# First query groups beside the even layer's last unit, a new order for the first unit, and later weight loads behind the y pieces

## The chip, the cores and the metric

One core of a Trainium2 chip runs the whole program in one launch. The metric is device time in microseconds. Engines are called as the profile calls them: PE (TensorE, matmuls), PEld (its weight loads), DVE (VectorE), ACT (ScalarE), POOL (GpSimd) and SP (SyncE, which issues nearly all DMAs). Every engine works through its own instructions in the order in which they were put, so an instruction that waits holds all that stand behind it.

## The reference

One inference step of two layers over a prompt of 2048 rows and 32 sample rows (8 sequences of 4 tokens), model width 1024, float32. Layer 0 runs HGRN2 heads and forgetting-attention heads in parallel from one input projection; layer 1 is gated linear attention.

```python
h = rmsnorm(x, norm_even)                   # layer 0
qa, fa, ia, ga, qb, kb, vb, gb, fb = split(h @ w_in_even)      # eight blocks of 512 columns, fb has 4
f = lb + (1 - lb) * sigmoid(fa)
o_a = gated_linear_chunked(qa, 1 - f, ia, log(f))              # 4 heads of 128, state in and out
o_b = forgetting attention (qb, kb, vb, log_sigmoid(fb + b_fox)):
    c = cumsum(log_f)
    prompt: softmax(q k^T * 128**-0.5 + c_t - c_s, s <= t) @ v          # 2048 queries, 4 heads
    sample: the same over 2048 paged past rows per sequence (128 pages of k, 128 of v) and 4 new ones
x = x + concat(head_rmsnorm(o_a) * silu(ga), o_b * silu(gb)) @ w_out_even
h = rmsnorm(x, norm_odd)                    # layer 1: GLA, 4 heads, key 128, value 256
x = x + (head_rmsnorm(gla(h @ w_in_odd)) * silu(g)) @ w_out_odd
y = rmsnorm(x, final_norm)
```

Outputs are y, the new keys, values and log forgets, and the states.

## The kernel before, in words

**Float32 from half-precision matmuls.** Every float32 operand is scaled by a power of two and split into a high and a low half in 16 bits; a product takes three matmuls (`mm3`, L476: hi·hi, hi·lo, lo·hi, lines 478 to 480). A weight unit is 256 columns: `half_unit` (L315) loads the raw block (`wr_…`), *measures* its largest value (four reduces `rm_…` on DVE, one small matmul `spr_…` that spreads it over the partitions, four tiny DVE steps), and *splits* it into `w_…` on ACT, DVE and POOL.

**Even layer** (`phase_even`, L958). The prompt is taken in two halves of 1024 rows; the sample's 32 rows go with the first. `norm_groups` (L408) loads row tiles (`nx_…`), squares them on ACT (`nsq`), scales them on DVE, transposes them on PE (`nt_…`) and splits the result into `act`. Then 16 units of projection per half run in a fixed order: v0, g0, qf0, qf1, …, Bk0, Bv0, Bk1, Bv1 (in the trace `pt_Av`, `pf_Ag`, `pf_A…`, …, `pt_Bk`, `pt_Bv`). `staged` (L1070) hands one unit's pieces to PE and between them fetches, measures and splits the units to come, by a list `todo`: for unit 0 of the first half it names unit 1's steps and, after the last piece, unit 2's measure, scale and split. `handover` (L452) mixes the norm of the row tiles with unit 0's pieces. `few_rows` (L510) does the sample's rows (`pS_…`) from a copy of their columns (`sam_…`, DVE). `more_consts` (L159) prepares constants (`lb`, `wgr`, `scT`, `mlev`) after unit 0. The linear attention of each head is mixed between pieces by `mux`, by costs that the code gives.

**Forgetting attention** (`phase_fox`, L1148). `bias_rows` writes the cumulated log forgets to `cbd`. `fox_prompt` (L1183) goes through 16 groups of 512 queries (4 heads × 4): per block of 128 queries scores `s` (PE), bias and running maximum (DVE, L1233), exponentials (ACT, L1241), normalising (POOL, L1249), transposes `pt` (PE, L1269), halves `th`/`tl` (ACT L1276, DVE L1277) and values `fo` (PE). The decode stream `fox_sample` (L1336) goes through the 256 pages (256 KB each): transposes `pkt`, copies `kts`, scores `sc`, softmax, values `pv`; its setup splits queries into `qz` on DVE. `until` (L92) alternates the two by the ratio of two numbers, `FOX_P` = 270000 for the prompt's cost and `FOX_S` = 411000 for the sample's, until the sample is through. What is left of the prompt is mixed with `prepare`, the odd layer's first loads.

**Odd layer** (`phase_odd`). `y_pieces` (L1608) load the attention output `yr` and split it into `act`; `row_tiles` load the rows `row_…` to which the output projection adds; `out_units` (units 0 to 3, `pt_o`) multiply by `w_out_even`, whose blocks are `wr_o`. Then norm and the units of layer 1.

**What sets the order.** The kernel records its operations in the order in which the generators yield, and a scheduling layer then places them per engine; inside `tc.issue_after(x)` an operation gets a place behind x. Tile pools give buffers by tag; a pool opened in the place of a closed one waits for its tiles.

## Time and profile before

| | us |
|---|---|
| median of 3 runs | 2395.92 (2392.24 to 2399.04) |
| the profiled execution, its own time | 2394.72 |
| its span, first to last instruction | 2392.4 |
| mean granted TensorE clock in it | 0.986 |

In the profile the even layer lies at 0 to 883 us, the forgetting attention at 883 to 1310, the rest to the end is the odd layer. A row of the timeline gives the start, the duration, engine, line, operation, output and inputs, their shapes, how many were merged, and in brackets how long the engine sat idle before it and what ended that. [...] A row of the busy time by stretch gives for each engine the us of work in the stretch and the instructions, then the granted clock as a share of full speed, the DMA engines' mean busy share and their GB/s.

### The profile page before, as it was taken

The numbers are of one execution on the slowest core, as the hardware profiler recorded it, in microseconds if no ns is written. First come the engines' busy times: TensorE is split into PE (matmuls) and PEld (weight loads), VectorE is DVE, ScalarE is ACT, GpSimd is POOL, SyncE is SP. The second block draws the span as 40 slices with busy tenths as digits, with TensorE's granted clock in tenths as the row PEclk, the third lists the DMA queues.
The fourth block names the chain that finished last, engine by engine and source line by source line (L and its number), as shares of the span: only waits on it lengthen the run. The fifth ranks groups of instructions, "written<-read, shape, count | busy, mean of one in ns | idle before, by whom it ended". The sixth has DMA issues, their size and how long they took to land. (4 is left out here: it accounts for less than half of the span.)

```text
span 2392.4 us, 58667 instructions
## 1 busy us (share of the span) xinstructions
PE 2294.1 (96%) x23324; PEld 1633.7 (68%) x23324; DVE 1417.9 (59%) x3347; ACT 1107.5 (46%) x2458; POOL 753.7 (32%) x843
## 2 busy tenths in 40 slices
PE   6999999999999999999999999999999999999998
PEld 5677677864655875655446876777778766666887
DVE  7566556446655548666767463665675645557554
ACT  5334343342333226556667454535543635545333
POOL 2233222112212225234556211432452222322322
PEclk9999999999999999999999999999999999999999
DMA  6231234535541267676874632122156312114453
GB/s 198 63 88 58 81 113 142 175 92 143 149 136 43 85 192 258 223 251 203 270 241 134 213 109 58 46 81 86 50 151 196 111 41 70 43 59 159 154 192 147
DMA packets 297013, 317.24 MB, mean 133 GB/s; under 512 B 39730, under 2 KB 241011, under 8 KB 296739
## 3 DMA queue, kind: packets, MB, share of 16 engines
q1 hardware_dynamic: 295234, 308.98, 41.1%
q8 instruction: 183, 3.00, 0.5%
q0 software_dynamic: 1504, 4.52, 0.5%
q14 instruction: 92, 0.75, 0.1%
HBM read 242.31 MB, written 71.11 MB: 131 GB/s over the span
## 5 line engine op out<-in xcount | busy, mean ns | idle before, releaser
L480 PE MATMUL pt_o<-w_o,act 128*128 128x256 f16 x1024 | 280.5, 274 | 3.1 <-DVE act L1633 2.9
L478 PE MATMUL pt_o<-w_o,act 128*128 128x256 f16 x1024 | 280.7, 274 | 1.3 <-ACT sg1C L534 1.1
L479 PE MATMUL pt_o<-w_o,act 128*128 128x256 f16 x1024 | 280.5, 274 | 1.0 <-POOL w_o L353 1.0
L480 PEld LDWEIGHTS <-act 128*128 128x128 f16 x2304 | 226.6, 98 | 36.1 <-issue 4.6
L478 PEld LDWEIGHTS <-act 128*128 128x128 f16 x2304 | 226.6, 98 | 36.0 <-ACT act L473 4.0
L479 PEld LDWEIGHTS <-act 128*128 128x128 f16 x2304 | 226.7, 98 | 32.4 <-issue 2.9
L478 PE MATMUL pt_Cv<-w_Cv,act 128*128 128x256 f16 (+1 forms) x512 | 140.3, 275 | 1.7 <-ACT act L473 0.9
L644 POOL TENSOR_TENSOR kA<-kA,fA 128x512 f32<-128x512 f32 (+1 forms) x56 | 79.8, 1425 | 192.6 <-PE gl_A L610 143.0
L479 PE MATMUL pt_Cv<-w_Cv,act 128*128 128x256 f16 (+1 forms) x512 | 140.0, 274 | 0.0
L480 PE MATMUL pt_Cv<-w_Cv,act 128*128 128x256 f16 (+1 forms) x512 | 139.7, 274 | 0.0
L1241 ACT ACTIVATE L<-L,nm,kc 128x512 f32<-128x512 f32 (+3 forms) x160 | 118.2, 741 | 36.9 <-DVE nm L1239 27.2
L644 POOL TENSOR_TENSOR kC<-kC,fC 128x512 f32<-128x512 f32 (+1 forms) x56 | 81.8, 1461 | 148.2 <-PE gl_C L610 101.3
L1249 POOL TENSOR_SCALAR L<-L,nm 128x512 f32<-128x512 f32 (+3 forms) x160 | 98.8, 631 | 70.8 <-DVE nm L1245 28.6
L1276 ACT ACTIVATE th<-pt 128x512 f16<-128x512 f32 (+3 forms) x159 | 80.7, 527 | 59.8 <-PE pt L1269 58.9
L1277 DVE TENSOR_TENSOR tl<-pt,th 128x512 f16<-128x512 f32 (+3 forms) x159 | 94.4, 609 | 20.3 <-ACT th L1276 19.0
L1269 PE MATMUL pt<-ident,L 128*128 128x128 f32 x544 | 91.3, 280 | 4.9 <-DVE tl L1277 2.4
L1269 PEld LDWEIGHTS pt<-ident,L 128*128 128x128 f32 x544 | 66.7, 143 | 32.4 <-DVE tl L1277 9.1
L1393 PEld LDWEIGHTS pkt<-ident,pgcache_fox_k 128*128 128x128 f32 x512 | 58.1, 141 | 44.4 <-issue 25.6
L1393 PE MATMUL pkt<-ident,pgcache_fox_k 128*128 128x128 f32 x512 | 76.1, 279 | 4.7 <-DVE kts L1397 2.0
L478 PE MATMUL pt_Av<-w_Ai,act 128*128 128x256 f16 x256 | 70.9, 277 | 1.9 <-ACT act L473 1.9
L479 PE MATMUL pt_Av<-w_Ai,act 128*128 128x256 f16 x256 | 70.7, 276 | 0.4 <-DVE w_Ai L346 0.4
L478 PE MATMUL pt_Bk<-w_Bk,act 128*128 128x256 f16 x256 | 71.0, 277 | 0.0
(952 smaller groups left out, 6738.3 us busy)
## 6 DMA issues: line engine op xcount, KB each, us to landing
pgcache_fox_k<-in_cache_fox_k SPq DMA_DIRECT2D x128, 256.0 KB, 4.2
pgcache_fox_v<-in_cache_fox_v SPq DMA_DIRECT2D x128, 256.0 KB, 4.2
yr<-yT SPq DMA_DIRECT2D x16, 1024.0 KB, 7.4
nx<-in_x_prompt SPq DMA_DIRECT2D x16, 512.0 KB, 5.4
wr_Aqf<-in_w_in_even SPq DMA_DIRECT2D x64, 128.0 KB, 3.2
wr_o<-in_w_out_even SPq DMA_DIRECT2D x32, 256.0 KB, 4.5
wr_Cv<-in_w_in_odd SPq DMA_DIRECT2D x32, 256.0 KB, 3.8
wr_Cqk<-in_w_in_odd SPq DMA_DIRECT2D x64, 128.0 KB, 2.8
```

Source lines behind the costliest of these rows:

```text
L478: nc.tensor.matmul(ps, lh[0], rh[0], start=first, stop=False)
L479: nc.tensor.matmul(ps, lh[0], rh[1], start=False, stop=False)
L480: return nc.tensor.matmul(ps, lh[1], rh[0], start=False, stop=last)
L644: nc.gpsimd.tensor_tensor(kv[:, :, 0], kv[:, :, 0], t1.to_broadcast([P, nb, w]), ALU.mult)
L1241: self.last_exp = nc.scalar.activation(lt[:, :w], lt[:, :w], AF.Exp, bias=nm[:, 0:1], scale=ib, accum_out=nm[:, 2 + j : 3 + j])
L1249: nc.gpsimd.tensor_scalar(lt[:, :w], lt[:, :w], nm[:, 1:2], 2.0**14, ALU.mult, ALU.mult)
L1269: nc.tensor.transpose(pt[:, w : w + P], rows[b][s // 4][0][:, (s % 4) * P : (s % 4 + 1) * P], self.ident)
L1276: nc.scalar.activation(th[:, a:w], pt[:, a:w], AF.Copy),
L1277: nc.vector.tensor_tensor(tl[:, a:w], pt[:, a:w], th[:, a:w], ALU.subtract)))
L1393: nc.tensor.transpose(pk[:, j * P : (j + 1) * P], pgs[j][:, h * P : (h + 1) * P], self.ident)
```

## The change

Four parts, in the diff's order of lines:

1. **Start.** `warm_up` puts matmuls of the identity with itself, into a PSUM tile that nobody reads, on PE: 9 behind `spr_e`, 4 behind the first transpose, one behind each second transpose of the first group of row tiles. The squares of every second row tile after the first group go to DVE. The row tile `nx_768` is loaded behind the first block `wr_Ag`. Unit 0 gives its first four pieces inside `handover`; then unit 1's first piece is taken (`next(gates)`), then the rest of unit 0. Unit 2's measure, scale and split, and steps of units 3 and 4, stand in unit 1's list; a scale step stands behind the last matmul recorded.
2. **Even layer's end.** `bias_rows` stands behind the second piece of unit Bk1 instead of behind the unit. The pools are split so that those on the left close early; `open_fox` opens the prompt's pools before the last unit Bv1, and `until` mixes prompt work of cost `PRE_P` = 16000 into Bv1's pieces. Two PSUM tags (`kt`, `sc`) are opened later, with the decode stream.
3. **`FOX_P`** is 245000 instead of 270000, so less prompt is handed out per decode step.
4. **Odd layer's start.** The weight loads of `dense(0, 3)` and the row tiles from the third on get a place behind the last load `yr`.

```diff
-FOX_P = 270000.0
+FOX_P = 245000.0
+PRE_P = 16000.0
...
-                    nc.scalar.activation(sq[:n], xt[:n], AF.Square, accum_out=ss[:n])
+                    if share and j and c0 > P:
+                        nc.vector.tensor_tensor_reduce(sq[:n], xt[:n], xt[:n], 1.0, 0.0, ALU.mult, ALU.add, ss[:n])
+                    else:
+                        nc.scalar.activation(sq[:n], xt[:n], AF.Square, accum_out=ss[:n])
...
+            def warm_up(n, after):
+                with tc.issue_after(after.ins):
+                    for _ in range(n):
+                        nc.tensor.matmul(warm[:, :P], self.ident, self.ident, start=True, stop=True)
+
+            warm_up(9, self.last_spread)
...
+                    def each0(st, k, j):
+                        if j or k == 0:
+                            warm_up(1 if j else 4, self.last_t)
+                        if (k, j) == (2, 0):
+                            st.enter_context(tc.issue_after(self.last_scale.ins))
...
-                    first = self.handover(list(zip(steps, turns)), dense(0, 1), last)
+                    first = dense(0, 1)
+                    drain(self.handover(list(zip(steps, turns)), islice(first, 4), last))
+                    gates = dense(1, 3)
+                    next(gates)
                     drain(first)
...
-                drain(dense(1, 3))
+                drain(dense(1, 3) if hf else gates)
...
-                drain(dense(14, 15))
+                keys = dense(14, 15)
                 if hf == 1:
+                    next(keys)
+                    next(keys)
                     self.bias_rows(pps, *masks)
+                drain(keys)
                 last = dense(15, 16)
-            drain(last)
+            left.close()
+            fx = self.open_fox()
+            drain(until(self.prompt, PRE_P, last, cost))
+        self.phase_fox(*fx)
...
+                    if n == 2:
+                        st.enter_context(self.tc.issue_after(self.last_mm.ins))
                     self.ready[u] = us[u][0][n]()
...
-            if j:
+            if j == 1 and beside:
+                todo = [[], [(2, 1), (4, 0)], [(2, 2)], [(2, 3), (3, 1)], [(3, 2)], [(3, 3)]]
+            elif j:
                 todo = [[(j + 3, 0), (j + 2, 1)], [(j + 2, 2)], [(j + 2, 3)]]
...
-                todo = [[(1, 0)], [(1, 1)], [(2, 0), (1, 2), (1, 3)], [(3, 0)], [(2, 1), (2, 2), (2, 3)]]
+                todo = [[(1, 0)], [(1, 1)], [(2, 0), (1, 2), (1, 3)], [(3, 0)]]
...
+                        if first and j > 1:
+                            st.enter_context(tc.issue_after(self.last_yr.ins))
+                        nc.sync.dma_start(t[:m], self.rows(hf, c0, m, first))
...
-            with tc.issue_after(self.last_y.ins):
+            with tc.issue_after(self.last_y.ins), tc.issue_after(self.last_yr.ins):
                 drain(dense(0, 3))
```

**PE, end of unit 0.** Before, the spread of unit 2's measure (`spr_Aqf`) stands between the sample's matmuls of unit 0 (`pS_Av`) and unit 1's first piece (`pf_Ag`):

```order
L522 MATMUL pS_Av_683<-w_Ai_153,sam_Av_680 32x256
L279 MATMUL spr_Aqf_721<-ident,rm_Aqf_715 128x128
L478 LDWEIGHTS w_Ag_577
L478 MATMUL pf_Ag_847<-act,w_Ag_577 128x352
L479 LDWEIGHTS w_Ag_577
```

Now unit 1's first piece begins among the last row tiles of unit 0, before the transposes of the sample's rows are through:

```order
L484 MATMUL pt_Av_648<-w_Ai_169,act 128x256
L483 LDWEIGHTS w_Ag_605
L483 MATMUL pf_Ag_709<-act,w_Ag_605 128x352
L484 LDWEIGHTS w_Ag_605
L484 MATMUL pf_Ag_709<-act,w_Ag_605 128x352
L445 MATMUL nt_2_624<-ident,nx_1024_509 128x32
```

The other 22 matmuls of that piece, the 24 of `pS_Av` and two more pieces (48 matmuls) then stand ahead of `spr_Aqf`.

**DVE, the same place.** Before:

```order
L517 COPY sam_Av_680<-act 128x8x32 x2
L292 TENSOR_REDUCE rm_Aqf_715<-wr_Aqf_560 128x1 x4
L165 TENSOR_SCALAR g_hgrn<-g_hgrn 128x4
L165 TENSOR_SCALAR g_gla<-g_gla 128x8
L172 TENSOR_TENSOR lb<-lb 128x4
L191 MEMSET wgr 80x512
L213 CAST mdiag<-ident 128x128
L232 MEMSET scT_833 128x1024
L232 MEMSET scT_834 128x1024
L292 TENSOR_REDUCE rm_Aqf_881<-wr_Aqf_671 128x1 x4
```

Now:

```order
L522 COPY sam_Av_738<-act 128x8x32 x2
L167 TENSOR_SCALAR g_hgrn<-g_hgrn 128x4
L167 TENSOR_SCALAR g_gla<-g_gla 128x8
L174 TENSOR_TENSOR lb<-lb 128x4
L193 MEMSET wgr 80x512
L215 CAST mdiag<-ident 128x128
L234 MEMSET scT_866 128x1024
L234 MEMSET scT_867 128x1024
L175 TENSOR_TENSOR lb<-lb 128x4
L176 TENSOR_TENSOR lb<-lb 128x4
L294 TENSOR_REDUCE rm_Aqf_908<-wr_Aqf_588 128x1 x4
L294 TENSOR_REDUCE rm_Aqf_997<-wr_Aqf_699 128x1 x4
```

Unit 2's reduces have moved behind the constants; seven more rows stand between them and the last small reduce that `spr_Aqf` takes.

**PE, the even layer's last unit.** Before, the first scores stand behind all of Bv1's matmuls:

```order
L480 MATMUL pt_Bv_10895<-w_Bv_10244,act 128x256
L478 LDWEIGHTS h_q_10986
L478 MATMUL s_11002<-h_k_10990,h_q_10986 128x128
L479 LDWEIGHTS h_q_10986
L479 MATMUL s_11002<-l_k_10991,h_q_10986 128x128
```

Now they stand inside, from behind its 54th matmul on:

```order
L485 MATMUL pt_Bv_11007<-w_Bv_10272,act 128x256
L483 LDWEIGHTS h_q_10790
L483 MATMUL s_10806<-h_k_10794,h_q_10790 128x128
L484 LDWEIGHTS h_q_10790
L484 MATMUL s_10806<-l_k_10795,h_q_10790 128x128
```

Counted over the whole order, the prompt's 1546 PE instructions (`s`, `pt`, `fo`) lie so, before and now: ahead of Bv1's last matmul 0 and 62; from there to the first `pkt` 62 and 85; from the first `pkt` to the last `pv` 1260 and 1161; behind it 224 and 238.

**SP, the odd layer's start.** Before (`yr` of 256 columns are 1 MB, `wr_o` and the rows 256 KB and 512 KB each):

```order
L1619 DMA yr_19220<-yT_76 128x8x256
L327 DMA wr_o_19432<-in_w_out_even 128x2x256 x4
L327 DMA wr_o_19542<-in_w_out_even 128x2x256
L1619 DMA yr_19437<-yT_76 128x8x256
L327 DMA wr_o_19542<-in_w_out_even 128x2x256 x3
L327 DMA wr_o_19611<-in_w_out_even 128x2x256 x4
L1619 DMA yr_19449<-yT_76 128x8x256
L1619 DMA yr_19461<-yT_76 128x8x32
```

Now:

```order
L1666 DMA yr_19183<-yT_76 128x8x256
L329 DMA wr_o_19462<-in_w_out_even 128x2x256 x4
L1666 DMA yr_19467<-yT_76 128x8x256
L1666 DMA yr_19479<-yT_76 128x8x256
L1666 DMA yr_19491<-yT_76 128x8x32
L329 DMA wr_o_19572<-in_w_out_even 128x2x256 x2
```

Seven loads `wr_o` stood ahead of the last `yr`; now only unit 1's four do, and the rows come ahead of the last six.

## Rows read from the trace of the kernel before

**Rows 1.** page, part 1: engine, busy us, share of the span, instructions

```profile
span 2392.4 us, 58667 instructions
PE 2294.1 (96%) x23324; PEld 1633.7 (68%) x23324; DVE 1417.9 (59%) x3347; ACT 1107.5 (46%) x2458; POOL 753.7 (32%) x843
```

**Rows 2.** timeline of PE, start: start, us, line, op, [idle before <-releaser]

```profile
8.12 1.11 PE L440 MATMUL nt<-ident,nx 128*128 128x128 f32 x4 [3.82 <-DVE nx L428]
15.85 0.42 PE L480 MATMUL pt_Av<-w_Ai,act 128*128 128x256 f16 x1
19.69 0.29 PE L480 MATMUL pt_Av<-w_Ai,act 128*128 128x256 f16 x1
21.34 0.27 PE L480 MATMUL pt_Av<-w_Ai,act 128*128 128x256 f16 x1
```

**Rows 3.** timeline of PE, end of unit 0 and start of unit 1

```profile
50.67 1.66 PE L522 MATMUL pS_Av<-w_Ai,sam_Av 128*32 128x256 f16 x24 [1.47 <-DVE sam_Av L517]
59.14 0.79 PE L279 MATMUL spr_Aqf<-ident,rm_Aqf 128*128 128x128 f32 x2 [6.82 <-DVE kc L261]
59.73 0.50 PE L478 MATMUL pf_Ag<-act,w_Ag 128*128 128x352 f16 x1
64.11 0.31 PE L478 MATMUL pf_Ag<-act,w_Ag 128*128 128x352 f16 x1
65.90 0.31 PE L478 MATMUL pf_Ag<-act,w_Ag 128*128 128x352 f16 x1
```

**Rows 4.** timeline of DVE beside it

```profile
50.39 0.83 DVE L517 COPY sam_Av<-act 128x256 f16<-128x256 f16 x2
50.73 2.45 DVE L292 TENSOR_REDUCE rm_Aqf<-wr_Aqf 128x1 f32<-128x512 f32 x4
56.08 2.39 DVE L292 TENSOR_REDUCE rm_Aqf<-wr_Aqf 128x1 f32<-128x512 f32 x4
58.95 0.14 DVE L294 TENSOR_REDUCE rm_Aqf<-rm_Aqf 128x1 f32<-128x4 f32 x1
```

**Rows 5.** timelines of DVE and ACT, norm of a row tile

```profile
19.95 0.75 DVE L428 TENSOR_SCALAR nx<-nx,rsr_n 128x1024 f32<-128x1024 f32 x1 [0.66 <-POOL rsr_n L405]
16.16 1.04 ACT L426 ACTIVATE nsq<-nx 128x1024 bf16<-128x1024 f32 x1
```

**Rows 6.** busy by stretch: us, PE PEld DVE ACT POOL, PEclk, DMA share, GB/s

```profile
883.20:901.30 18.10, 14.59 (x65) 7.26 (x63) 12.45 (x55) 10.07 (x26) 11.73 (x19) 0.72 0.95 311
901.30:914.30 13.00, 8.90 (x48) 4.55 (x47) 10.28 (x28) 8.46 (x21) 8.63 (x11) 0.87 0.97 335
914.30:1272.70 358.40, 343.15 (x2441) 196.76 (x2442) 248.64 (x769) 229.09 (x517) 161.94 (x258) 0.99 0.71 231
1272.70:1310.30 37.60, 33.13 (x239) 24.39 (x239) 30.55 (x85) 27.49 (x60) 30.41 (x35) 0.95 0.30 98
```

**Rows 7.** timeline of PE, from the even layer into the forgetting attention

```profile
883.18 0.27 PE L480 MATMUL pt_Bv<-w_Bv,act 128*128 128x256 f16 x1
900.13 0.39 PE L1269 MATMUL pt<-ident,L 128*128 128x128 f32 x2
900.35 0.22 PE L479 MATMUL fo<-tl,h_v 128*128 128x128 f16 x1
901.33 1.04 PE L1393 MATMUL pkt<-ident,pgcache_fox_k 128*128 128x128 f32 x8
909.04 0.22 PE L478 MATMUL s<-h_k,h_q 128*128 128x128 f16 x1 [2.41 <-DVE mx L1233]
```

**Rows 8.** timeline of DVE beside it

```profile
905.74 2.64 DVE L1385 TENSOR_TENSOR qz<-qs,bmask 128x256 f32<-128x256 f32 x4
```

**Rows 9.** timeline of SP's queue, start of the odd layer

```profile
1304.89 7.28 SPq L327 DMA_DIRECT2D wr_o<-in_w_out_even  x7
1313.39 5.76 SPq L1619 DMA_DIRECT2D yr<-yT  x2
```

**Rows 10.** busy by stretch, start of the output projection's second unit

```profile
1330.00:1340.00 10.00, 8.96 (x97) 7.42 (x96) 8.21 (x15) 7.19 (x15) 7.53 (x6) 1.00 1.07 349
```

More of the change, by code (lines that the diff above doesn't have):

```diff
@@ L1 @@
 from contextlib import ExitStack
+from itertools import islice
 import concourse.bass as bass
@@ L262, in spread @@
         ps = pps.tile([P, 512], F32, tag=tag, name=f"spr_{nm}")
-        nc.tensor.matmul(ps[:, :P], m.to_broadcast([P, P]), self.ident, start=True, stop=True)
+        self.last_spread = nc.tensor.matmul(ps[:, :P], m.to_broadcast([P, P]), self.ident, start=True, stop=True)
         nc.vector.reduce_max(t, ps[:, :P], axis=mybir.AxisListType.X)
@@ L429, in prep, with turn @@
                     xs.append(xt)
-            def turn(at=None, then=None):
+            def turn(each=None):
                 c0 = grp[0][0]
@@ L438, in turn @@
                         w = 0
-                        for (_, n), xn in zip(grp, xs):
-                            nc.tensor.transpose(ps[:, w : w + n], xn[:n, k * P : (k + 1) * P], self.ident[:n, :n])
+                        for j, ((_, n), xn) in enumerate(zip(grp, xs)):
+                            self.last_t = nc.tensor.transpose(ps[:, w : w + n], xn[:n, k * P : (k + 1) * P], self.ident[:n, :n])
                             w += n
+                            if each:
+                                each(st, k, j)
                         self.split_evac(ps[:, :w], act[0][:, k, c0 : c0 + w], act[1][:, k, c0 : c0 + w],
                                         gain[:, k : k + 1])
-                        if k == at:
-                            then(st)
             return prep, turn, load
@@ L485, in proj_fm @@
             for k in range(KT):
-                self.mm3(ps[:M, :n], [x[:, k, off : off + M] for x in W],
-                         [x[:, k, c0 : c0 + n] for x in act], k == 0, k == KT - 1)
+                self.last_mm = self.mm3(ps[:M, :n], [x[:, k, off : off + M] for x in W],
+                                        [x[:, k, c0 : c0 + n] for x in act], k == 0, k == KT - 1)
             evac(ps[:M, :n], c0, n)
@@ L971, in phase_even @@
             self.sx_even = self.gain_scale(self.g_even, pps, "pj", "e")
+            warm = pps.tile([P, 512], F32, tag="st", name="warm")
+            def warm_up(n, after):
[3 more added lines that the diff above has]
+            warm_up(9, self.last_spread)
             S1 = sp.tile([P, P], F32, name="Sx")
@@ L1018, in behind, with turn @@
                             groups[g][0]()
[L1020 to L1029 removed]
+                    def each0(st, k, j):
[3 more added lines that the diff above has]
+                            st.enter_context(tc.issue_after(self.last_scale.ins))
+                    def turn0():
+                        groups[0][1](each0)
+                    def turn(t):
+                        groups[t][1](lambda st, k, j: behind(self.last_a, t + 1) if (k, j) == (KT // 2, 0) else None)
+                    steps = [lambda: None, lambda: behind(self.last_split, 1), lambda: None, lambda: None, lambda: None]
+                    turns = [turn0] + [lambda t=t: turn(t) for t in (1, 2, 3)] + [groups[4][1]]
+                    first = dense(0, 1)
+                    drain(self.handover(list(zip(steps, turns)), islice(first, 4), last))
+                    gates = dense(1, 3)
+                    next(gates)
                     drain(first)
+                    first = iter(())
                     with tc.issue_after(self.last_x.ins), tc.issue_after(self.last_a.ins), \
@@ L1146, in log_sigmoid, with open_fox @@
         nc.vector.scalar_tensor_tensor(zz, q, -2.0, zz, ALU.mult, ALU.add)
[L1148 removed]
+    def open_fox(self):
         tc, nc = self.tc, self.nc
         self.fox = ExitStack()
[L1151 to L1164 removed]
@@ new lines, in pool @@
+        def pool(name, **kw):
+            return self.fox.enter_context(tc.tile_pool(name=name, bufs=2, reuse_waits="tile", **kw))
+        f1, f0, pp = pool("fe"), pool("fx"), pool("fpa", space=PSUM)
+        fx = Pool(f0, {"vh": 5, "vl": 5, "P": 17, "th": 4, "tl": 4, "sg": 3, "y": 1},
+                  Pool(f1, {"raw": 6, "caus": 1, "qh": 2, "ql": 2, "kh": 5, "kl": 5, "cb": 2, "st1": 12, "cm": 2}))
+        more = Pool(None, {"kt": 2, "sc": 1})
+        pps = Pool(pp, {"t": 2, "o": 1, "s": 2}, more)
@@ new lines, in open_fox, with phase_fox @@
+        caus = fx.tile([P, P], F32, tag="caus", name="caus")
+        nc.gpsimd.memset(caus, 0.0)
+        nc.gpsimd.affine_select(caus, caus, [[-1, P]], ALU.is_ge, FAR, base=0, channel_multiplier=1)
+        self.prompt = self.fox_prompt(fx, pps, caus)
+        return pps, more
+    def phase_fox(self, pps, more):
+        tc = self.tc
+        more.pool = self.fox.enter_context(tc.tile_pool(name="fpb", bufs=2, space=PSUM, reuse_waits="tile"))
+        with tc.tile_pool(name="fs", bufs=1, side="right", reuse_waits="tile") as s0:
+            fs = Pool(s0, {"pg": PG, "kt": 8})
+            drain(until(self.prompt, FOX_P, self.fox_sample(fs, pps), FOX_S))
@@ L1862, in row_tiles @@
                     t = wp.tile([P, HALF + TS], F32, tag="c4" if j < OC4 else "sg", name=f"row{hf}_{j}")[:, :D]
-                    nc.sync.dma_start(t[:m], self.rows(hf, c0, m, first))
+                    with ExitStack() as st:
+                        if first and j > 1:
+                            st.enter_context(tc.issue_after(self.last_yr.ins))
+                        nc.sync.dma_start(t[:m], self.rows(hf, c0, m, first))
                     r.append(t)
```

48 lines of the change are left out of this document (15 added, 33 removed).

## The prediction

> **What bounds the kernel now.** [...] A matmul of 256 columns costs 0.213 us at the lower level (18 steps from 15.85 to 19.69) and 0.110 at the upper one (15 steps to 21.34) [rows 2]. Three places stand out. At the start PE waits 3.82 us for the first row tile and begins unit 0 at the lower level [rows 2]. At the end of unit 0 it waits 1.47 us for `sam_Av`, then 6.82 us at `spr_Aqf`, and unit 1 begins at the lower level: 0.292 us a matmul of 352 columns for 15 steps, then 0.149 for 12 [rows 3]. Between the even layer and the decode stream the granted clock is 0.72 for 18 us and 0.87 for 13 more [rows 6], with a wait of 2.41 us in them [rows 7]. Beside the decode stream PE is busy 343.15 of 358.4 us, DVE 248.64, ACT 229.09, the DMA engines 0.71 [rows 6]: PE is the limit there, nothing else is near.
>
> **Part 1, the start.** *The stall.* `spr_Aqf` needs the last reduce of unit 2's measure, which DVE ends at 59.09 after working since 50.39 on the sample's copies, eight big reduces and the constants between them [rows 4]. The change does not shorten that work; it puts it behind other PE work. DVE's 8.7 us from the copies to that reduce become about 10 (the order shows `wg`, a sum and unit 1's first product ahead of it now; I put 1.3 on them, about two steps of a 128x512 reduce at 0.6 [rows 4]). PE has in that time `pS_Av` (1.66) and 48 matmuls of 0.149, so 1.66 + 7.15 = 8.8 us, beginning 0.3 us behind the copies. So PE arrives some 0.9 us early: of 1.47 + 6.82 = 8.29 us I take 1 as coming back, 7.3 are won (5.8 to 8.3). The 22 matmuls of unit 1's first piece ahead of `pS_Av` (3.3 us) cover the 1.47.
> *The clock behind it.* Without the stall the 15 slow steps cost 15 x (0.292 − 0.149) = 2.1 us less (0 to 2.1): the clock fell in that stall and in nothing else near it.
> *The warm-up.* Nine identity products are two passes each of 0.213 us at the lower level, 3.8 us in all, beside a wait of 3.82 [rows 2]: they delay nothing. In the two places where a lower clock rose it did so 4 to 5 us after dense work had begun (15.85 to 19.69, 59.73 to 64.11) [rows 2, 3], so it should be up by about 9 to 10 us, ahead of unit 0. The 18 slow steps then give 18 x 0.103 = 1.9 us at most. Against it: the second group's tile `nx_384` now has its squares on DVE ahead of its scaling. No row shows that operation there. The nearest are DVE's scaling of such a tile, 0.75, and ACT's square of it, 1.04 [rows 5]; I take 1.1, as it reads two operands, which puts that tile about 1 us later. And if the clock is not up by then, four products of 0.43 stand ahead of `spr_Ai`, to which the first weights are tied. I take 1.0 won (−2 to 1.9). The squares on DVE further on, 3 in all, and `nx_768` behind `wr_Ag` lie beside unit 0, where PE has 36 us of its own work; without that cover they would cost 3.3.
> Sum of part 1: 7.3 + 2.1 + 1.0 = **10.4 us won** (4 to 12).
>
> **Parts 2 and 3, the way into the decode stream.** I price the prompt's PE instructions by the steps above, in proportion to columns (512: 0.216, 384: 0.163, 256: 0.109, 128: 0.056), and a transpose at 0.11 (two from 900.13 to 900.35) [rows 7]. By the counts of the order that gives, before and now: in Bv1 0 and 9.0 us; from Bv1's end to the first `pkt` 9.0 and 14.9; beside decode 199.0 and 181.9; behind the last `pv` 28.5 and 30.7.
> - Bv1 grows by 9.0, and by 1.0 more for waits (0 to 4): every unit of scores is followed by six or more `pt_Bv` that need nothing from it.
> - From Bv1's end (883.18) to the first `pkt` (901.33) [rows 7] were 18.15 us for 9.0 us of work, a ratio of 2.0, much of it the clock. Behind the last `pv` the prompt again runs without decode: 37.6 us [rows 6] for 28.5, a ratio of 1.32. Bounds for the 14.9 us now standing alone: no waits 14.9, ratio 2.0 30.0. I take 1.32, since that stretch, like the new one, begins in flow (loads made, clock up): 19.7, that is 1.5 more than before (−3.2 to +11.8).
> - DVE's setup of the decode queries (`qz` alone 2.64 us [rows 8]) holds the prompt's maximum, PE waits 2.41 [rows 7], and 13% of the 13 us run slow for it (1.7 us): 4.1 us. The setup stays, but more of the prompt's work is then ahead of it on PE. I take half, 2.1 won (0 to 4.1).
> - Beside decode 17.1 us of PE work go, where PE is busy 96%: 17.1 won (0 only if something else were the limit).
> - Behind the last `pv` 2.2 more at a ratio of 1.32: 2.9 lost (2.2 to 4.4).
> Sum: −10.0 − 1.5 + 2.1 + 17.1 − 2.9 = **4.8 us won** (13.8 won to 12 lost). `bias_rows` two pieces earlier costs its two small matmuls wherever they stand; it only brings `cbd` earlier.
>
> **Part 4.** `yr` (256 columns) waits behind seven `wr_o` of 256 KB [rows 9], at the 349 GB/s of that stretch [rows 10] 5 us. The unit's weights are split on ACT behind the y pieces, and PE, 8.96 busy of 10 us there [rows 10], waits for them: 1.04 us, all that is to be won. With the rows ahead of the last six `wr_o` (rows 4 MB, 12 us), units 2 and 3 get their weights about 12 us later, but PE reaches them 23 and 46 us behind unit 1 (192 matmuls of 0.11 and the sample's in each unit). **1.0 won** (0 to 1.5).
>
> **Sum.** 10.4 + 4.8 + 1.0 = 16.2 us off the profiled execution's 2394.72: 2378.5, so **2378 us**, 18 below the median of 2395.92; the profiled execution is 1.2 below that median.
>
> **The rivals.**
> - *The stall only moves.* DVE's chain is as long as before; if the products of unit 1 or the constants hold it 5 us longer than I take, PE waits at `spr_Aqf` 6 us instead of 1, the clock falls again (2.1), and the time is 2378 + 7 = **2385**. For it: DVE worked without a gap there [rows 4]. Against: PE has 8.8 us of work that needs none of it.
> - *The prompt alone runs at the lower clock again.* If the 14.9 us stand at the ratio 2.0 of rows 6 and 7, the term is 10.3 worse: 2378 + 10 = **2388**. For it: the DVE and POOL waits inside that stretch are of the softmax, which is no shorter now, and the clock was 0.72 there with PE busy 14.59 of 18.1. Against: that stretch began with the first loads of the forgetting attention and unsplit queries, which now lie beside Bv1. [...]
> - *Slower: the softmax chain sets the prompt's pace, not PE.* Then prompt work in the decode stream is only filler, and taking 17.1 us out of it saves nothing there, while every us of it put elsewhere is paid: Bv1 10, alone 11.8, tail 2.9, no setup won, against 11.4 from parts 1 and 4: 2394.7 + 24.7 − 11.4 = **2408**. It decides once the decode stretch gives back less than 13 of the 17. Against: PE's 96% and DVE's 69% there.
> - *All waits go.* Warm start full, setup free, the prompt alone at ratio 1: 12 + 13.8 + 1.5 = 27, **2367**. For it: ACT and DVE are busy 10.07 and 12.45 of 18.1 us [rows 6], so they would have room if PE went on.
>
> **How the numbers follow.** Forecast 0.50 (its own range 2371 to 2386), stall moved 0.12, alone at the lower clock 0.18, slower chain 0.05, all waits gone 0.15. About 0.3%, 7.2 us, is what a measurement of this kernel tells from no change. Below 2388.7 lie the forecast, the last rival, most of the first (0.10) and half of the second: 0.85 faster. From there to 2403.1 lies the rest of both: 0.10. Above it the chain: 0.05. Leaving out the chain and outer tails of the two ends, the range is 2366 to 2391.
>
> **What would show it.** Right: PE's step 0.11 from unit 0's first matmuls on; no idle time above 2 us at `spr_Aqf` and unit 1 at 0.149 throughout; scores among `pt_Bv`; at most 20 us from Bv1's end to the first `pkt` with the clock above 0.9; the stretch from the first `pkt` to the last `pv` about 19 us shorter (17.1 + 2.1); no wait for `w_o` at unit 1 of the output projection. Wrong: a wait of 5 us at `spr_Aqf`; a clock near 0.7 behind Bv1 again; a decode stretch shorter by under 13 us; PE idle for `w_o` of units 2 and 3.

## The result and the profile after

The changed kernel took **2405.93 us**, median of 8 runs (2401.89 to 2408.93), beside 2395.97 (2392.24 to 2399.15) of the kernel before on the same chip: a ratio of **1.0045**, 95% interval 1.0032 to 1.0058. It is 10 us slower where 18 us faster was forecast. The profiled execution took 2407.4 us. The page's first part answers to [rows 1]:

```profile
span 2405.7 us, 58751 instructions
PE 2302.4 (96%) x23366; PEld 1641.3 (68%) x23366; DVE 1422.7 (59%) x3353; ACT 1105.7 (46%) x2452; POOL 757.2 (31%) x843
```

PE's idle time went from 98.3 to 103.3 us and its busy time grew by 8.3. Cut at the same tiles, the two profiled executions give (us):

| stretch | before | after |
|---|---|---|
| start: to the first `pf_A00f` (unit 2) | 83.6 | 83.4 |
| even layer from there to the end of Bk1 | 777.4 | 779.3 |
| Bv1 | 22.2 | 30.4 |
| Bv1's end to the first `pkt` | 18.1 | 18.6 |
| decode: first `pkt` to last `pv` | 371.8 | 368.0 |
| rest of the prompt, to the first `pt_o` | 37.2 | 42.5 |
| first `pt_o` to the first `pt_Cv` | 90.6 | 89.6 |
| from there to the start of PE's last matmul | 982.0 | 985.1 |
| from there to the end of the span | 9.5 | 8.8 |

**Start.** The stall of [rows 3] is gone, and the start is as long as before. PE's timeline, unit 0 and unit 1 (columns as in [rows 2]; "..." leaves rows out; the durations are longer than the steps: one of 0.27 us at 15.74 is followed by the next at 15.85):

```profile
24.26 0.28 PE L483 MATMUL pt_Av<-w_Ai,act 128*128 128x256 f16 x1 [0.86 <-ACT act L478]
...
28.11 0.28 PE L485 MATMUL pt_Av<-w_Ai,act 128*128 128x256 f16 x1 [0.94 <-DVE act L479]
...
29.59 0.77 PE L445 MATMUL nt<-ident,nx 128*128 128x128 f32 x2 [0.98 <-DVE nx L433]
...
52.20 0.28 PE L483 MATMUL pt_Av<-w_Ai,act 128*128 128x256 f16 x1 [1.22 <-ACT act L478]
...
71.36 0.38 PE L281 MATMUL spr_Aqf<-ident,rm_Aqf 128*128 128x128 f32 x2
```

`spr_Aqf` waits for nothing, but stands at 71.36 where it stood at 59.14. Unit 0 now has the waits: this and the following views show why. ACT in the kernel before, then in the change, and DVE in the change:

```profile
23.18 1.57 ACT L473 ACTIVATE act<-nt,g_even 128x256 f16<-128x256 f32 x4 [4.12 <-PE nt L440]
```

```profile
23.00 0.84 ACT L822 ACTIVATE v<-pt_Av,kc 128x256 f32<-128x256 f32 x2 [5.28 <-PE pt_Av L485]
23.73 1.57 ACT L478 ACTIVATE act<-nt,g_even 128x256 f16<-128x256 f32 x4
```

```profile
26.44 1.21 DVE L429 CUSTOM_DVE_ANT_0 nsq<-nx 128x1024 bf16<-128x1024 f32 x1
27.58 0.08 DVE L429 DVE_READ_ACCUMULATOR2_ANT nss<- 128x1 f32 x1
27.58 0.48 DVE L479 SCALAR_TENSOR_TENSOR act<-nt,g_even,act 128x256 f16<-128x256 f32 x1
28.61 0.16 DVE L263 TENSOR_REDUCE kc<-g_odd 128x1 f32<-128x8 f32 x1 [0.55 <-DMA g_odd<-in_norm_odd]
28.69 0.76 DVE L433 TENSOR_SCALAR nx<-nx,rsr_n 128x1024 f32<-128x1024 f32 x1
```

In the change ACT stands 5.28 us with the evacuation `v` (the copy of a finished piece out of PSUM) at the head of its queue until PE has ended that piece, and the next group's splits `act` are behind it; in the kernel before it stands 4.12 us there, but the splits are at the head and start as soon as the transposes `nt` are done. DVE puts a square of 1.21 us ahead of the scaling `nx`, for which PE waits at 29.59. The busy time by stretch (columns as in [rows 6]) of the kernel before, of the change, then of a kernel with the early gates alone (below; "gates" are unit 1, `pf_Ag`):

```profile
30.00:40.00 10.00, 9.83 (x87) 8.73 (x88) 8.56 (x21) 7.95 (x19) 1.63 (x3) 1.00 0.79 203
40.00:50.00 10.00, 9.19 (x75) 6.97 (x72) 6.13 (x23) 8.06 (x22) 1.94 (x2) 1.00 0.03 10
```

```profile
30.00:40.00 10.00, 8.62 (x60) 6.64 (x60) 4.30 (x10) 4.58 (x12) 1.46 (x2) 0.84 0.84 219
40.00:50.00 10.00, 8.39 (x67) 6.53 (x67) 8.66 (x27) 4.53 (x12) 1.58 (x3) 1.00 0.03 10
50.00:60.00 10.00, 7.78 (x44) 4.45 (x45) 5.13 (x15) 5.97 (x16) 3.67 (x5) 0.83 0.31 88
```

```profile
30.00:40.00 10.00, 10.00 (x83) 9.01 (x81) 8.41 (x20) 7.73 (x18) 1.63 (x3) 0.88 0.83 209
40.00:50.00 10.00, 10.00 (x84) 7.85 (x81) 6.80 (x24) 7.08 (x19) 0.97 (x1) 1.00 0.06 19
50.00:60.00 10.00, 10.00 (x87) 6.41 (x86) 8.71 (x26) 4.46 (x12) 3.20 (x5) 1.00 0.40 117
```

**Boundary, decode and rest.** The change, by stretch (Bv1 from inside, boundary, decode, rest), answers to [rows 6]:

```profile
883.00:893.10 10.10, 10.10 (x79) 7.50 (x78) 7.16 (x29) 5.48 (x16) 3.40 (x7) 1.00 0.23 77
893.10:911.70 18.60, 16.64 (x88) 8.35 (x87) 16.83 (x61) 15.84 (x40) 15.40 (x25) 1.00 0.84 266
911.70:1279.70 368.00, 337.64 (x2393) 192.93 (x2391) 240.86 (x734) 221.02 (x494) 158.09 (x248) 0.98 0.72 230
1279.70:1322.20 42.50, 38.45 (x252) 27.85 (x245) 33.97 (x88) 28.47 (x61) 28.42 (x31) 0.85 0.27 86
```

The boundary has the length and the clock that were forecast: 18.6 us, at 1.00 instead of 0.72. But the clock is not what had made it long. part4_loads (below), whose order of instructions there is that of the kernel before, was granted 1.00 in the same stretch and took 17.9 us, against 18.1 at 0.72:

```profile
879.00:896.90 17.90, 11.59 (x66) 5.72 (x64) 12.39 (x55) 10.14 (x27) 11.76 (x19) 1.00 0.99 321
```

So the 9.0 us of prompt work had long waits there at either level, and the 1.00 can't be put down to part 2 by these executions alone. In decode PE was busy 352.05 of 371.4 us [rows 6] and is now 337.64 of 368.0. So of 17.1 us of prompt work taken out, 14.4 left its busy time and 11.0 of these came back as idle time (19.4 to 30.4). What PE waited for there, before and after (total us, times, longest):

```profile
PE s L478 <- DVE mx L1233: 3.7, 4, 2.4
...
PE pkt L1393 <- DVE kts L1397: 2.0, 4, 0.9
...
PE psf L1442 <- ACT lfTs L1441: 0.2, 1, 0.2
```

```profile
PE pv L1579 <- DMA pgcache_fox_v<-in_cache_fox_v: 3.8, 3, 1.6
PE s L483 <- DVE mx L1280: 3.7, 7, 1.0
PE pkt L1440 <- DVE kts L1444: 3.2, 8, 0.8
...
PE psf L1489 <- ACT lfTs L1488: 2.7, 1, 2.7
```

The long wait for `mx` has become several short ones. The wait of `pv` for its pages' loads is new, and that of `psf` for the pages' transposed log forgets (`lfTs`) has grown from 0.2 to 2.7 us. Summed over the whole view, PE's waits at the decode stream's own instructions grew from 6.2 to 14.6 us, those at the prompt's from 11.9 to 14.5. At the end of decode the clock falls (the change, around the last `pv` at 1279.7, and in the rest):

```profile
1275.00:1280.00 5.00, 3.16 (x19) 0.98 (x17) 2.30 (x5) 3.17 (x9) 3.95 (x7) 0.90 0.00 0
1280.00:1285.00 5.00, 5.00 (x19) 2.69 (x16) 4.14 (x8) 1.20 (x2) 0.00 (x0) 0.50 0.00 0
...
1300.00:1305.00 5.00, 1.99 (x14) 1.28 (x14) 5.00 (x11) 5.00 (x11) 5.00 (x6) 0.79 0.00 0
1305.00:1310.00 5.00, 4.95 (x25) 4.06 (x25) 2.80 (x6) 3.92 (x10) 4.96 (x7) 0.53 0.08 3
```

At 0.50 a matmul of 512 columns stands 0.43 us behind the one before it (1282.35 to 1282.78), ahead of the fall 0.21 (1278.37 to 1278.58); the slow steps of [rows 3], granted 0.50 as well, have about the same ratio to the fast ones, 0.292 to 0.149. It comes behind 5 us in which PE worked 3.16, and a second time while DVE, ACT and POOL are busy 5.00 of 5 and PE 1.99.

### The profile page after: what moved, and what is told of

It reads as the page before. It is cut to its first block, busy times and chain, and to the rows that moved or that the text cites. A ratio compares the mean times of both kernels' runs of the same rounds, so it can differ in the third digit from the quotient of the medians.

```text
span 2405.7 us, 58751 instructions
## 1 busy us (share of the span) xinstructions
PE 2302.4 (96%) x23366; PEld 1641.3 (68%) x23366; DVE 1422.7 (59%) x3353; ACT 1105.7 (46%) x2452; POOL 757.2 (31%) x843
## 5 line engine op out<-in xcount | busy, mean ns | idle before, releaser
L1324 DVE TENSOR_TENSOR tl<-pt,th 128x512 f16<-128x512 f32 (+3 forms) x159 | 94.1, 608 | 28.1 <-ACT th L1323 26.8
L1316 PEld LDWEIGHTS pt<-ident,L 128*128 128x128 f32 x544 | 67.5, 145 | 34.4 <-DVE tl L1324 10.4
L483 PE MATMUL pt_Av<-w_Ai,act 128*128 128x256 f16 x256 | 70.9, 277 | 4.9 <-ACT act L478 4.9
L485 PE MATMUL pt_Av<-w_Ai,act 128*128 128x256 f16 x256 | 70.9, 277 | 3.2 <-DVE act L479 3.2
L484 PE MATMUL pt_Av<-w_Ai,act 128*128 128x256 f16 x256 | 70.8, 277 | 0.6 <-DVE w_Ai L348 0.6
```

The costliest lines, as they stand in the source:

```text
L483: nc.tensor.matmul(ps, lh[0], rh[0], start=first, stop=False)
L484: nc.tensor.matmul(ps, lh[0], rh[1], start=False, stop=False)
L485: return nc.tensor.matmul(ps, lh[1], rh[0], start=False, stop=last)
L1316: nc.tensor.transpose(pt[:, w : w + P], rows[b][s // 4][0][:, (s % 4) * P : (s % 4 + 1) * P], self.ident)
L1324: nc.vector.tensor_tensor(tl[:, a:w], pt[:, a:w], th[:, a:w], ALU.subtract)))
```

## The experiments

Sixteen kernels, each timed beside the kernel before, whose median was 2394.3 to 2396 in every batch. Spans and clocks of single executions differ by up to 15 us, so a second account stands beside the medians: each execution's span times its mean granted clock, averaged over a kernel's executions, is the time it would have taken if every stretch had shrunk in proportion to its clock (**full-clock time**); the remainder of the span is **lost to the clock**. It is an upper bound: the boundary of the kernel before (18.1 us at 0.72) counts 5.1 us as lost, and part4_loads, granted 1.00, got back 0.2 of them there, for PE waits in both (3.5 and 6.3 us). The slow steps of [rows 2] are not in it: the profile has 1.00 for them. The full-clock time of the kernel before itself differs by batch, 2367.3, 2364.5, 2366.1 and 2366.7; the table has the last, and a sum has to take each kernel's own batch.

| kernel (runs) | median | ratio, interval | full-clock | clock |
|---|---|---|---|---|
| before (22, last batch) | 2395.87 | | 2366.7 | 27.1 |
| the change (8) | 2405.93 | 1.0045, 1.0032 to 1.0058 | 2374.8 | 28.8 |
| part1_start (12) | 2400.78 | 1.0018, 1.0004 to 1.0033 | 2369.0 | 29.6 |
| start_no_dve_squares (12) | 2393.77 | 0.9995, 0.9984 to 1.0006 | 2366.4 | 25.7 |
| start_gates_warm (12) | 2391.57 | 0.9986, 0.9976 to 0.9995 | 2360.3 | 28.3 |
| start_gates_only (6) | 2383.79 | 0.9957, 0.9942 to 0.9972 | 2361.0 | 21.0 |
| start_squares_only (10) | 2395.99 | 1.0003, 0.9992 to 1.0014 | 2368.0 | 26.3 |
| start_warm_only (4) | 2409.32 | 1.006, 1.0042 to 1.0078 | 2373.1 | 33.1 |
| part23_boundary (6) | 2410.35 | 1.006, 1.0042 to 1.0079 | 2376.6 | 31.3 |
| part2_foxp270 (6) | 2411.69 | 1.0062, 1.0039 to 1.0086 | 2380.8 | 28.1 |
| part2_same_rest (12) | 2393.75 | 0.9992, 0.998 to 1.0003 | 2370.1 | 21.3 |
| part3_foxp245 (6) | 2408.62 | 1.0063, 1.0047 to 1.0078 | 2377.4 | 28.5 |
| part4_loads (12) | 2392.75 | 0.9992, 0.9979 to 1.0005 | 2365.9 | 24.5 |
| gates_and_loads (6) | 2385.38 | 0.9958, 0.9942 to 0.9973 | 2360.2 | 23.4 |
| gates_loads_foxp285 (12) | 2393.12 | 0.9994, 0.9983 to 1.0006 | 2365.7 | 25.7 |
| after_old_unit0 (10) | 2398.58 | 1.0008, 0.9994 to 1.0021 | 2370.3 | 26.6 |
| after_old_unit0_foxp248 (7) | 2385.93 | 0.9956, 0.9939 to 0.9974 | 2365.1 | 17.7 |

decode_alone was run once (2533.43 us).

### The parts alone

**part1_start, part23_boundary, part4_loads, part2_foxp270.** The diff of the change cut to part 1, to parts 2 and 3, to part 4, and to part 2 alone (`FOX_P` left at 270000).

> Only part 1 (the start) on the kernel before. Theory A: the stall at spr_Aqf goes, but the new order of the norm in unit 0 makes PE wait as much again (after: nine waits of 0.4 to 1.3 us between 15 and 54 us and a stretch at half clock from 29.6 to 33), so the first matmul of unit qf0 begins at 83.4 us as in before (83.6) and the time is 2395 to 2397. Rival B: part 1 wins its 10 us and something later in the program gives them back: then it begins before 76 us here and the time is about 2386.

> Only parts 2 and 3 (queries beside Bv1, FOX_P 245000) on the kernel before. Theory A: these carry the whole loss: Bv1 8 to 9 us longer, the decode stretch only about 4 us shorter although 17 us of prompt work went out of it, the rest of the prompt 5 longer: 2405 to 2408. Rival B (the loss is elsewhere, in the odd layer's start or the late odd layer): 2393 to 2398.

> Only part 4 (weight loads behind the last yr) on the kernel before. Theory: the last yr lands 5 us earlier, PE's wait of 1 us at unit 1 of the output projection goes: 2394 to 2395.5. Rival: units 2 and 3 then wait for their weights: 2397 or more with PE idle for w_o after 1357 us.

> Part 2 with FOX_P back at 270000. The decode stretch then has as much prompt work beside it as in before, and the prompt's rest behind it is about 15 us of PE work shorter. Theory A (prompt work beside decode is filler in PE's waits): the decode stretch stays at about 371 us, the rest of the prompt falls from 37 to about 18 us, Bv1 is 9 longer: 2385 to 2390. Rival C (decode is limited by PE, FOX_P is indifferent): 2403 to 2408 as with 245000. Rival D (the rest of the prompt is limited by the odd layer's first loads and splits, not by PE): the rest stays above 30 us and the time is 2400 or more.

Part 1 alone has the start of the change (83.5 us), as expected by theory A, but is 6 us slower instead of even. Parts 2 and 3 alone have a boundary of 19.6 us, decode of 371.8 (PE idle 31.7) and a rest of 42.8 and are slower by more, 2 us past the expected range. Part 4 alone gives 88.6 for 90.6 between the first `pt_o` and the first `pt_Cv`. The wait for `w_o` of 1.0 us there is gone, but kernels without part 4 have 88.4 to 90.5 in that stretch (88.4 part1_start, 89.2 start_gates_warm, 90.5 start_squares_only), so no gain is shown. Part 2 with the old `FOX_P` takes 14.6 us of work out of the rest of the prompt (13.9 instead of 28.5) and loses them twice: the boundary is 30.6 us, and the odd layer's first pieces stand uncovered, as PE's waits from 1290 to 1420 show (first `pt_o` to first `pt_Cv` 102.5 us); none of its three theories fits whole:

```profile
PE pt_o L483 <- ACT act L1657: 6.2, 1, 6.2
PE pt_o L485 <- POOL act L1655: 3.6, 2, 2.7
```

### The start taken apart

**start_gates_only** keeps of part 1 only the early first piece of unit 1 and, behind it, unit 2's measure and the steps of units 3 and 4; **start_gates_warm** adds the identity products.

```
-                    first = self.handover(list(zip(steps, turns)), dense(0, 1), last)
+                    first = dense(0, 1)
+                    drain(self.handover(list(zip(steps, turns)), islice(first, 4), last))
+                    gates = dense(1, 3)
+                    next(gates)
                     drain(first)
+                    first = iter(())
...
+                todo = [[], [(2, 1), (4, 0)], [(2, 2)], [(2, 3), (3, 1)], [(3, 2)], [(3, 3)]]
```

> Of part 1 only the move of unit 2's measure and of unit 1's first piece; the row tiles' squares, loads and turns and PE's start as in before (no identity products). Theory A1 (the new order of the row tiles is what costs, not the move): PE idles as little in 15 to 50 us as in before (1.7 us), the stall of 6.8 is gone, and unit qf0 begins at 74 to 77 us instead of 83.6; the time is 2386 to 2389. Rival A2 (DVE's and ACT's chain for the weights of unit 2 is the limit, wherever PE stands): it still begins at 82 to 84.

> The same with the identity products. If the clock at unit 0's start is worth what its slow steps cost: qf0 1 to 2 us earlier than without them. If the row tiles set the pace of unit 0 (their squares, scaling and splits): 0 to 0.5 earlier, with PE idle in 20 to 40 us longer by what the clock won.

The move alone takes 10.1 us out of the start (83.6 to 73.5), with PE busy throughout from 30 to 60 us (view above) and a wait of 0.2 at `spr_Aqf`. The five kernels with this start and no products have 72.5 to 73.5 us, the seven with the old one 82.9 to 84.5, so the gain repeats; the 73.0 of the kernel with the products lies inside that spread. The medians are 7.8 us apart, the full-clock times 0.7. The difference lies behind the start, where the sources are the same but the programs are not: the traces show DVE's instructions in another order around 900 us and from 1180 to 1230 us (an example from start_warm_only is below).

**start_no_dve_squares** is part 1 with `share=False`; **start_squares_only** is the kernel before with `share=hf == 0`; **start_warm_only** adds only the identity products.

> All of part 1 but the squares on DVE (they stay on ACT). Theory S (the squares on DVE hold the scaling of the second tile of each group): PE's waits in 15 to 54 us fall from 9 to under 4 us and qf0 begins at 74 to 77 us. Theory T (the new turns, one group's preparation in the middle of the turn before, two groups later than it was, are what costs): qf0 begins at 80 to 85 us, as with the squares on DVE.

> Only the squares of every second row tile of the first half on DVE; no identity products, no early gates. Theory A (ACT's v and act splits, DVE's nx behind the square, starve unit 0): the start grows from 83.6 us by 3 to 8 us and waits of 0.5 to 1.4 us stand in unit 0; median 2398 to 2404. Rival (the squares cost only together with the new turns and the early gates): start within 2 us of 83.6, median within 3 us of before. The prediction's term: 1 us.

> Only the identity products at the start; orders of units 0 to 2, squares and everything later as before. Theory A (the time behind the start depends on the phase at which the clock falls, by several us, whatever the edit): the start, now 83.6 us, moves by no more than 2 us, yet the median differs from the kernel before by 3 us or more in either direction, with the difference in stretches whose program is unchanged. Theory B (the products cost the 7.8 us by which the kernel with them and the early gates is slower than the one without): slower by 5 us or more, in the start. Theory C (the prediction's term): 1 to 2 us faster, all of it in the start.

With the squares back on ACT the start of part 1 falls from 83.5 to 76.7 us; the old turns of the next groups (start_gates_warm) give the remaining 3.7. The squares alone cost 2.8 us of start (86.4), of which the median shows nothing. So the squares cost 6.8 us in the new order and 2.8 in the old, neither of my two guesses exactly. The stall has not swallowed the other 4: in start_squares_only it takes about the same time as in [rows 3], so what makes the squares dearer in the new order is open:

```profile
PE spr_Aqf L281 <- DVE rm_Aqf L296: 7.2, 1, 7.2
```

start_warm_only edits nothing behind the start, whose length it leaves at 83.1, and is 13 us slower. Decode takes 375.4 us (3.6 more), the rest 33.9 (3.3 less), the first units of the output projection 98.8 (8.2 more), with a wait that the kernel before has for 0.8 us at most (PE's waits from 1308 to 1408):

```profile
PE pt_o L483 <- ACT w_o L354: 3.8, 1, 3.8
```

That is the wait that part 4 is made against. It was not tried with part 4 added. Theory A asked for differences where the program is unchanged, but there the order has changed: the scheduling layer has placed later instructions otherwise. DVE at the same softmax step, in the kernel before and in start_warm_only:

```profile
898.91 0.17 DVE L1245 RECIPROCAL nm<-nm 128x1 f32<-128x1 f32 x1
898.99 0.47 DVE L1233 CUSTOM_DVE_ANT_0 L<-s,cb,mx 128x256 f32<-128x256 f32 x1
...
899.38 0.62 DVE L1277 TENSOR_TENSOR tl<-pt,th 128x256 f16<-128x256 f32 x2
```

```profile
897.27 0.16 DVE L1266 RECIPROCAL nm<-nm 128x1 f32<-128x1 f32 x1
897.35 0.42 DVE L1298 TENSOR_TENSOR tl<-pt,th 128x256 f16<-128x256 f32 x1
897.69 0.47 DVE L1254 CUSTOM_DVE_ANT_0 L<-s,cb,mx 128x256 f32<-128x256 f32 x1
```

The half `tl` now stands ahead of the maximum `mx`. More such exchanges, on ACT and POOL too, lie between 1225 and 1340 us, and six of the prompt's matmuls moved from behind the last `pv` to ahead of it. In part4_loads, edited only at the odd layer's start, DVE, ACT and POOL keep the order of the kernel before up to 1300 us. So an edit of the start also brings another order of the forgetting attention, and a median holds both; which exchange made decode longer is open.

### How decode and the prompt share PE

**part3_foxp245** is the kernel before with `FOX_P` 245000; **part2_same_rest** is part 2 with `FOX_P` 248000, which leaves 28.5 us of prompt work behind the last `pv` as before; **decode_alone** takes the prompt out of decode:

```
-FOX_P = 270000.0
+FOX_P = 1.0
...
-            drain(mux(self.prompt, REST_P, prepare(), REST_S))
+            drain(self.prompt)
+            drain(prepare())
```

> Only FOX_P 245000 on the kernel before: some 20 us of prompt work move from beside decode to behind it. Theory F (prompt work beside decode only fills PE's waits): the decode stretch stays at 369 to 373 us, the rest of the prompt grows from 37 to about 58 to 62 us: 2410 to 2418. Rival G (PE is the limit beside decode): decode falls by 15 to 20 us, the rest grows by as much and a little more: 2396 to 2401.

> Part 2 with FOX_P 248000, so that the prompt's rest behind the decode stream is 28.5 us of PE work as in before; 9.0 us stand in Bv1, 14.9 ahead of the first pkt, 184.1 beside decode. By the price read from decode with 11, 182 and 199 us of prompt work (264, 364.5 and 371.8 us: about 0.55 us for a us of it), decode falls by 15 x 0.45 to 0.55 = 7 to 8; Bv1 costs 8.2, the way to the first pkt 1.5, setup nothing: 2 to 4 us slower than before, 2396 to 2400. If beside decode PE were the limit: 7 faster.

> The decode stream with next to no prompt beside it (FOX_P 1, the prompt drained after it and before the odd layer's first loads; longer in all). How long is the stretch from the first pkt to the last pv? Theory F: not much shorter than the 372 us with 199 us of prompt work in it: 300 to 360. Rival G: decode's own PE work alone, about 157 us (busy 356 less 199), with some waits: 160 to 220.

Decode and the rest in decode_alone, by stretch, and its longest wait:

```profile
895.50:1159.60 264.10, 184.53 (x1293) 82.69 (x1295) 75.31 (x206) 59.18 (x113) 22.84 (x35) 0.82 0.83 266
1159.60:1450.10 290.50, 252.24 (x1486) 155.44 (x1479) 221.65 (x715) 218.66 (x509) 182.50 (x265) 0.93 0.30 95
```

```profile
PE pv L1532 <- DMA pgcache_fox_v<-in_cache_fox_v: 50.9, 23, 3.5
```

Decode with 11 us of prompt work takes 264 us, of which PE is idle 80, most of it for the pages' loads. With 182 to 184 us of prompt work it takes 361.5 to 372.5 (six kernels), with 199 it takes 371.0 to 375.4, with 209 (gates_loads_foxp285) 383.7. So from 11 to 199 us of work each us cost on average (371.8 − 264.1) / 188 = 0.57 us of decode time, while alone behind it each cost 290.5 / 224.6 = 1.29. The average is not the price at every point: the last 9.5 us, from 199.5 to 209, cost 11.3. And part of it is the clock: decode nearly alone was granted 0.82, beside the prompt 0.99, and its own PE work took some 173.5 us (184.5 busy less 11) instead of some 153.5 (352.5 less 199), as the prediction prices the prompt's work. Against the kernel before, 15 to 17 us taken out gave between −0.7 and 10.3 us back, and part3_foxp245 paid for them behind it: decode −7.3, rest +25.5 (62.7 us).

part2_same_rest came out between its two expectations. It has the change's boundary at FOX_P 248000, 2.2 us of prompt work more ahead of the last `pv`. Boundary, decode and rest by stretch:

```profile
890.20:908.80 18.60, 16.64 (x88) 8.35 (x87) 16.82 (x61) 15.83 (x40) 15.37 (x25) 1.00 0.90 286
...
908.80:1272.30 363.50, 338.77 (x2407) 194.88 (x2405) 241.76 (x738) 220.62 (x496) 157.46 (x248) 0.98 0.71 231
1272.30:1309.50 37.20, 31.27 (x238) 23.23 (x231) 30.70 (x84) 26.74 (x58) 28.03 (x31) 1.00 0.30 97
```

The rest is at full clock and 37.2 us, and the median 16.6 below part23_boundary.

### Place or chance, and the best version

**gates_and_loads** is start_gates_only with part 4; **gates_loads_foxp285** has `FOX_P` 285000 besides. **after_old_unit0** is the whole change with only the early gates of part 1; **after_old_unit0_foxp248** has `FOX_P` 248000 besides.

> What the runs so far leave of the change: the move of unit 2's measure and of unit 1's first piece, and part 4; no identity products, squares and turns as before, no queries beside Bv1, FOX_P 270000. If the two add up (10.4 and 2 us): 2381 to 2384.

> The same with FOX_P 285000: 10 us of prompt work more beside decode, the rest 18.9 instead of 28.5 us. By the prices so far decode grows by 4 to 5, the rest shrinks by 12 to 13: 7 to 9 us faster than with 270000, if the odd layer's first loads and splits still fit beside the rest. If they don't (theory D): PE idles for act at the first pt_o and the time is the same or longer.

> The whole change (FOX_P 245000) with the start reduced to the early gates: no squares on DVE, no identity products, old turns. If the start is one of two independent losses: start 73 us instead of 83.4, median 2396 (10 below the change's 2406), and the rest behind the last pv 42 us as in the change. If the time won at the start is lost again later: start 73 us, median 2402 or more.

> The kernel above with FOX_P 248000. If the 16 us between 245000 and 248000 seen with the old start are of the place (2.2 us of prompt work more ahead of the last pv): 2380 to 2386, the stretch behind the last pv 37 us at clock 1.00, below both kernels. If they were of the phase: within 5 us of the kernel above, and the stretch behind the last pv not shorter by more than 3.

More prompt in decode (285000) is no gain either: decode +11.3, rest −8.8, and the odd layer's first units +8.1, for they have only 18.9 us of prompt work to hide behind (PE waits there for `act`, at most 1.9 us, where gates_and_loads has no such wait). after_old_unit0 is 7.3 us below the change: the start was one of the losses. 3000 less in `FOX_P` parts the last two kernels by 12.7 us, as it parted part23_boundary and part2_same_rest by 16.6, so the step is not chance: it comes with `FOX_P` on two bases. In the profiled executions 11.0 and 8.3 us of it lie in decode and 6.2 and 5.6 behind the last `pv`; the place at which decode ends can explain the latter, the part inside decode is open. Decode and rest of after_old_unit0, then of after_old_unit0_foxp248:

```profile
897.20:1269.70 372.50, 340.26 (x2389) 193.97 (x2391) 241.00 (x736) 221.17 (x494) 157.66 (x249) 0.97 0.69 225
1269.70:1313.00 43.30, 38.10 (x251) 27.65 (x244) 34.25 (x88) 29.81 (x63) 28.42 (x31) 0.87 0.27 86
```

```profile
900.40:1261.90 361.50, 336.39 (x2407) 193.83 (x2405) 241.78 (x738) 221.19 (x496) 157.97 (x248) 0.99 0.71 232
1261.90:1299.00 37.10, 31.26 (x237) 23.25 (x230) 30.66 (x84) 26.20 (x57) 27.85 (x30) 1.00 0.30 97
```

Three kernels are 10 us below the kernel before: start_gates_only, gates_and_loads and after_old_unit0_foxp248, 2383.8 to 2385.9, which their intervals do not tell apart.

Do the parts add up? Beside the kernel before of their own batches, in full-clock time and as medians, the kernels with one part give: part 1 +1.7 and +6.0, parts 2 and 3 +9.3 and +15.6, part 4 −1.4 and −2.0. The sums are +9.6 and +19.6, and the change was measured at +8.1 (beside the last batch) and +10.0: the full-clock times come near, the medians do not. In finer steps both come near: early gates −3.5 and −10.5; squares, products and new turns (the change less after_old_unit0) +4.5 and +7.4; part 2 with a matched rest +4.1 and −1.2; `FOX_P` from 248000 to 245000 (mean of the two pairs) +5.2 and +14.7; part 4 −1.4 and −2.0; in all +8.9 and +8.4. But one of these steps is taken from the change itself, so this sum proves less than the first.

## Why the prediction was wrong, step by step

In the change the start won 0.2 us where 10.4 were forecast, and the way from Bv1 to the end of the prompt lost 10.2 where 4.8 were to be won.

- **The stall at `spr_Aqf`: right.** Forecast 7.3 us and 2.1 of clock behind it; the move alone took 10.1 us out of the start.
- **"The squares on DVE further on, 3 in all, and `nx_768` behind `wr_Ag` lie beside unit 0, where PE has 36 us of its own work": wrong.** This is the first step that failed: the overlap. PE's work in unit 0 takes its input from ACT and DVE row tile by row tile, and it hid none of this: the squares cost 6.8 us in the new order and the new turns with `nx_768` 3.7 (not parted further). The square itself, priced 1.1, took 1.21 and 0.08, so that price was nearly right; but the cover was not there, and the 3.3 that the prediction gave for having no cover is a third of what was lost.
- **The warm-up, 1.0: right in kind.** In the change the nine products behind `spr_e` took 18 instructions of 0.214 us (4.21 to 8.07), as the prediction has them, and unit 0 went at 0.11 from step to step from 15.63 on, where the kernel before took 0.213 up to 19.69. The 0.5 us by which the start is shorter lie inside the spread of equal starts.
- **Bv1 +10.0: a little high,** 8.2. **Alone 19.7: right in length,** 18.6 us from Bv1's end to the first `pkt`, at clock 1.00, but the reason was not: the prediction put much of the old 18.15 us down to the clock, and part4_loads took 17.9 with the clock at 1.00. What the setup's 2.1 gave was not measured by itself; the longest wait for `mx` fell from 2.4 to 1.0. Whether short waits of PE bring the clock down is not settled by the rows: with waits of 0.5 to 1.3 us unit 0 of the change was granted 0.84 from 30 to 40 us with PE busy 8.62, but start_no_dve_squares 1.00 with PE busy 8.50; the boundary of the change, at 16.64 busy of 18.6, was granted 1.00, and so was that of part4_loads at 11.59 of 17.9.
- **"Beside decode 17.1 us of PE work go, where PE is busy 96%: 17.1 won": wrong,** the second step that failed. The prediction read PE's busy share as PE being the limit. The 96% held because the prompt filled the pauses of a stream that waits on its own pages and copies: in decode_alone PE waits 50.9 us for the pages of `pv` and 19.1 for the copies `kts`. With 17.1 us of filler less, 11.0 us became pauses and 3.8 were won. The other five kernels with 182 to 184 us of prompt work in decode lie between 0.7 lost and 10.3 won, all under 13. "0 only if something else were the limit" was the bound to take seriously.
- **Behind the last `pv` −2.9: too small,** −5.3. The 2.2 us were priced by a mean ratio; the place at which decode ends counts as well: behind the last `pv` the three kernels with the change's part 2 and `FOX_P` 245000 were granted 0.85 to 0.87, the two with 248000 1.00.
- **Part 4, 1.0: the wait for `w_o` went, a gain is not shown,** as kernels without part 4 spread over 2 us in that stretch (start_warm_only, with its longer wait, lies 8 above them).

The rival "slower: the softmax chain sets the prompt's pace", put at 0.05 and 2408, gave the sign and nearly the time, and its condition came true: decode gave back 3.8 of 17, under 13. Its mechanism is half right: prompt work in decode is filler, but of the 11 us of waits that take its place some 8 belong to the decode stream and under 3 to the prompt's softmax, the boundary was not slow as it had it, and the total is near by luck: it counted 24.7 us of loss in the parts that lost 10.2, and 10.4 us of gain at the start that did not come.

## What to carry to other kernels

A busy share of 96% does not tell that taking work out saves as much time: where one of two mixed streams paces itself, ask what each us costs there (0.57 on average here) and what it costs elsewhere (1.29) before moving it. When a stall is removed by reordering, make that move by itself first; the additions around it (squares on another engine, other turns) took back all of it here. Compare several executions by span and granted clock. Compare the order of the engines' instructions behind the edited place as well, for the scheduling layer can change it hundreds of us later; and treat a single kernel's gain of a few us as unproven until the same edit has shown it from two bases.
